# Reordering around three seams of a macaron trunk: weight casts ahead of squares, a scan product ahead of a mix, decay products behind the state sums

## The chip, the core and the metric

The kernel runs on one core of a Trainium2 chip, as one program. The metric is device microseconds of one execution; the time before is the median of three runs. Besides, one execution was recorded by the hardware profiler; its lines are shown below as they were printed.

The engines are called by the profile's names: PE is TensorE's matmuls and PEld its weight loads, DVE is VectorE, ACT is ScalarE, POOL is GpSimd, SP is SyncE, which issues most of the transfers.

## What is computed

Two layers over a sequence of 512 rows of width 1024. Each layer is a macaron: half a SwiGLU, a mixer, half a SwiGLU, each behind an RMSNorm. The mixer of layer 0 is a Mamba-2 SSD, that of layer 1 is an S5 state-space model. A final RMSNorm ends it.

```python
for i in range(2):
    x = x + 0.5 * swiglu(rmsnorm(x, ffn1_norm[i]), ffn1_w_in[i], ffn1_w_out[i])
    h = rmsnorm(x, mix_norm[i])
    m = ssd_mixer(h, ...) if i == 0 else s5_mixer(h, ...)
    x = x + m
    x = x + 0.5 * swiglu(rmsnorm(x, ffn2_norm[i]), ffn2_w_in[i], ffn2_w_out[i])
return rmsnorm(x, final_norm)

# SSD, per chunk, in 8 groups of 4 heads
decay = exp(where(causal, cs[t] - cs[s], -inf))
y_diag = einsum(cb * decay, dtx)
y_off = einsum(c, state) * exp(cs)
new_state = state * exp(cs[-1]) + einsum(b, exp(cs[-1] - cs) * dtx)

# S5: 64 groups of width 16, 64 complex states each
states = scan(lam_bar, b_bar u);  y = Re(c states) + d u
out = (gelu(y) @ W_val + b) * sigmoid(gelu(y) @ W_gate + b)
```

## The kernel before

Activations are kept transposed, eight tiles `xT[d]` of 128 channels by 512 positions. Every float32 product is made from high and low halves: a weight tile of up to 1024 x 128 is fetched to `wst`, ScalarE casts its high half `whi` (L226), VectorE subtracts it for the low half `wlo` (L228), and `proj` issues three matmuls for each 128 rows (L235 to L237). Activations are split the same way into `hH` (L173) and `hL` (L182), or `ah` and `al`. There are three buffers each for `whi` and `wlo`, four for `wst`.

The program runs six stages one after the other: `f1_0`, `ssd`, `f2_0`, `f1_1`, `s5`, `f2_1`. A planner orders the instructions of each engine by the order in which they are written and by its own estimate of when each is ready. Inside a `manual_schedule` region the engines that it names keep the written order; a nested region orders only those that the outer one doesn't. `keep_in_program_order` pins one instruction behind the one written before it on its engine. TensorE is in written order everywhere around the change.

**The feed-forward stage `ffn7`** (`f2_0`, `f1_1`, `f2_1`) takes the 22 tiles of the hidden width in five parts. Each part ends in an output pass over the eight `d`: `part` issues the projection into `pos[d]`, `split` prepares the weight of two steps on, `fetch_to` asks for later ones, and `after(d)` adds half of the result to `xT[d]` (L597, or L594 with `turn`, which writes it transposed for S5). In the last part `after` also calls the next stage's `Prep.take`: it makes `hH` and the square `sq` (L160) on ScalarE, and leaves for one step later (`held`) a `rest` that makes `hL` and adds the square to `acc` (L167) on VectorE. `pop` runs one closure of the list `fill`. In `f1_1` the last eight closures and those left over load and prepare what S5 needs: `scan_ops` (operators `opH` and tables `tb`), `out_ops` (`opP`), `u_load` (the vectors `U`, written out by `s5_sink` and read back regrouped), `res_load` (four gate weights) and `res_w`, which casts (L1381) and subtracts (L1389) such a weight. Then come the sums over channels (L137, or L198 ahead of S5) and the Newton steps of the inverse root (L121 to L128).

In `ffn7` the main loop is in written order on all five engines; the weights split ahead of that loop, and the seam between two stages, are the planner's.

**The SSD stage** treats eight groups `g`; only TensorE is in written order. For each group `states` forms three chunk states: matmuls (L847), a copy (L851), and two times a product with the decay (L853) and a sum (L857). `exps` makes the exponentials on ScalarE (L881), `decay(e)` multiplies them by `cb` on VectorE (L888, once for each pair of heads), and `outp(e)` uses the states (L897) and the decay products (L904) on TensorE. In the last group these steps are run between the steps of `out_rows`, the output projection (L779).

**The S5 stage** has TensorE, SP and GpSimd in written order. Its channels lie in eight blocks `i`. `states(i)` scales `U` by the norm (L1407) and multiplies by `opH` (L1413) into a PSUM tile; `swap(i)` copies its halves crosswise on ScalarE (L1424, L1425); `scan(i)` is three elementwise steps (L1433 to L1435), the scan (L1437), two copies (L1441, L1442) and three more steps (L1443 to L1445) that give `v`; `mix(i, h, w)` multiplies blocks `i` and `i + 1` by `opP` (L1454), with `w = 128` from `U` and with `w = 0` from `v`; `channels(i)` transposes the gelu of the result (L1474) and splits it (L1478, L1479); `glu_k` and `glu_out` are the gate. There are four PSUM tiles `aux` for `states`, `mix` and `channels`.

Of the kernel before, what the change touches and what calls it, by code (L numbers as in the profile page):

```python
# [13 lines left out]
OP = mybir.AluOpType  # L14
AX = mybir.AxisListType

T = 512
D = 1024
KD = 8
# [3 lines left out]
NG = 8  # L23
# [7 lines left out]
def trunk_kernel(ctx, tc, x, ffn1_norm, ffn1_w_in, ffn1_w_out, mix_norm, ffn2_norm, ffn2_w_in, ffn2_w_out,  # L31
# [189 lines left out]

        return split_w(fetch_w(src, kt, eng)[0], kt)

    def split_w(st, kt):
        hi = wpool.tile([128, KD, 128], F32R, name="whi", bufs=3)[:, :kt]
        S.copy(hi, st)  # L226
        lo = wpool.tile([128, KD, 128], F32R, name="wlo", bufs=3)[:, :kt]
        V.tensor_tensor(lo, st, hi.bitcast(F32), op=OP.subtract)  # L228
        return hi, lo

    def proj(ps, w, H, L, first=True, last=True):
        hi, lo = w
# [71 lines left out]
    def ffn7(pr, w_in, w_out, nxt, parts, fill=(), late=None, ring=None, pad=40, turn=None, after_w=(), have=None):  # L304
# [20 lines left out]
        def fetch_to(j):  # L325
            while len(raws) < min(j + 1, len(items)):
                raws.append(fetch_w(*items[len(raws)])[0])

        def split(j):
            if j < len(items) and j not in whole:  # L330
                fetch_to(j)
                whole[j] = split_w(raws[j], items[j][1])

        sevens = list(range(parts[0][1], FT))
        es = ExitStack()
# [197 lines left out]
        with tc.manual_schedule(engines=ALL):  # L533
            todo = []

            def pops(n):
                for _ in range(n):
                    todo and todo.pop(0)()

            for p, (a, b) in enumerate(parts):  # L540
                out = AH, AL = [], []
                prev = None
                for f in range(a, b):
                    if p:
                        iteration(f, prev, b, out)
                        prev = pairs[f]
                        continue
                    pg, pu = mm_ps(), mm_ps()
                    proj(pg, whole[2 * f], pr.H, pr.L)
                    split(2 * f + 2)  # L550
                    fetch_to(2 * f + 5)
                    gt, up = sv.tile([128, T], F32, name="gt"), sv.tile([128, T], F32, name="up")
                    if f == 0:
                        pr.sums()
                    else:
                        pops((0, 1, 2, 2, 2)[f])
                        V.tensor_tensor(gt, pg, pr.rbc, op=OP.mult)
                        S.activation(gt, gt, AF.Silu)
                    proj(pu, whole[2 * f + 1], pr.H, pr.L)
                    split(2 * f + 3)  # L560
                    fetch_to(2 * f + 6)
                    if f == 0:
                        pr.finish()
                        V.tensor_tensor(gt, pg, pr.rbc, op=OP.mult)
                        S.activation(gt, gt, AF.Silu)
                        for k in range(4):
                            todo += build(k)
                    else:
                        pops((0, 2, 2, 2, 0)[f])
                    V.tensor_tensor(up, pu, pr.rbc, op=OP.mult)  # L570
                    gated(up, 1.0, gt, out)
                    pop()
                n = b - a
                last = b == FT
                pos, held = [], []
                steps = {}
                if not last:
                    def step(name):
                        return lambda: getattr(pairs[b], name)()
                    if p == 0:  # L580
                        new_pair()
                        new_pair()
                    steps = {0: ["five"], 3: ["add7", "six"], 4: ["s6", "add3"], 7: ["s12"]}

                def part(d, k0, k1):
                    h, lo = whole[at[p, d]]
                    proj(pos[d], (h[:, k0:k1], lo[:, k0:k1]), AH[k0:k1], AL[k0:k1], first=k0 == 0, last=k1 == n)

                def after(d):
                    pops(1)  # L590
                    if last and turn:
                        new = s5.pop("spare", None) or turn()
                        pv, xv = [a_.rearrange("p (k q) -> p k q", q=8) for a_ in (pos[d], xT[d])]
                        V.scalar_tensor_tensor(new.rearrange("p (q k) -> p k q", q=8), pv, 0.5, xv, op0=OP.mult, op1=OP.add)  # L594
                        s5["spare"], xT[d] = xT[d], new
                    else:
                        V.scalar_tensor_tensor(xT[d], pos[d], 0.5, xT[d], op0=OP.mult, op1=OP.add)  # L597
                    if last:
                        held.append(nxt.take(d, hold=True))
                        if d:  # L600
                            held.pop(0)()
                    for nm in steps.get(d, ()):
                        getattr(pairs[b], nm)()
                    if last:
                        nxt.flush(3)
                    pop()

                for d in range(KD):
                    j = at[p, d]
                    pos.append(mm_ps())  # L610
                    if d == 0:
                        part(0, 0, 1)
                        if prev:
                            prev.acc_u4()
                            prev.c22()
                        split(j + 2)
                        if prev:
                            mul(prev.A, prev.W[3], 6)
                            prev.silu0()
                            prev.silu1()  # L620
                            mul(prev.E, prev.W[4], 0)
                            prev.c21()
                            gated(prev.up, -1.0, prev.gt, out)
                            if last:
                                es7.close()
                                fetch_to(j + 4)
                                if late:
                                    late()
                        part(0, 1, n - 1)
                        continue  # L630
                    if d == 1:
                        part(1, 0, n - 1)
                        for e in range(2):
                            part(e, n - 1, n)
                        split(j + 2)
                        fetch_to(j + 5)
                        for e in range(2):
                            after(e)
                        continue
                    part(d, 0, n)  # L640
                    if d < KD - 1 or last:
                        split(j + 2)
                    fetch_to(j + 5)
                    after(d)
                pops(len(todo))
                if last:
                    held.pop(0)()
            while fill:
                fill.pop(0)()
            nxt.flush()  # L650
            if nxt.kind != "hilo":
                nxt.sums()
                nxt.finish()
# [4 lines left out]
    def ssd(pr, nxt):  # L658
        w_in, w_out = ssd_in_proj[0], ssd_out_proj[0]
        with ExitStack() as es:  # L660
# [147 lines left out]
            def scan(g, BT, CT, XS, SZ):  # L808
# [76 lines left out]
                def decay(e):  # L885

                    m = st["M", e]
                    V.tensor_tensor(m, m, st["cb"][:, None, :].to_broadcast([128, 2, T]), op=OP.mult)  # L888

                def outp(e):  # L890
                    M = st["M", e]
# [500 lines left out]
    def res_w(j):  # L1392
        res_hi(j)
        res_lo(j)

    def s5_stage(pr, nxt):
        with ExitStack() as es:
# [124 lines left out]
            scan_ops(3, 1)  # L1522
            scan_ops(2, 2)
            scan(1)
            for i in (4, 5):
                u_load(i)
                scan_ops(i, 1)
            scan_ops(3, 2)
            out_ops(2, 0)
            scan_ops(4, 2)  # L1530
            states(2)
            for h in range(2):
                mix(0, h, 0)
            states(3)
            swap(2)
            swap(3)
            next_out(2)
# [62 lines left out]
        return rows  # L1600


    op_es = ExitStack()

    def prep_for(st):
        if st is None:
# [107 lines left out]
    for i, s in enumerate(stages[:-1]):  # L1714
# [9 lines left out]
        else:  # L1724
            L = int(s[-1])
            wi, wo = (ffn1_w_in, ffn1_w_out) if s[:2] == "f1" else (ffn2_w_in, ffn2_w_out)
            if s in s5_pre[:1]:
                ffn(pr, wi[L], wo[L], nxt, fill=pre0, ready=ready, done=done, early=early, pad=160)
                pre_es.close()
            elif s in s5_pre:  # L1730
                with tc.manual_schedule(engines=MAN):
                    have = ffn7(pr, wi[L], wo[L], nxt, ((0, 5), (5, 9), (9, 13), (13, 17), (17, 22)),
                                after_w=[(ffn1_w_in[1][:, c:c + 128], KD) for c in (0, FF)])
            elif stages[i + 1] == "s5":
# [4 lines left out]
                    G.memset(s5["sel"].rearrange("p (a b) -> p a b", b=8)[:, :, 7:8], 1.0)  # L1739
                    out_ops(0, 0)  # L1740

                fill = [lambda: None] * 63
                fill[52] = lambda: (scan_ops(0, 2), scan_ops(1, 1))
                fill[53] = lambda: scan_ops(1, 2)
                fill[54] = lambda: out_ops(1, 0)
# [4 lines left out]
                fill[59] = lambda: (res_load(3), res_w(1))  # L1750
                fill[60] = lambda: u_load(2)
                fill[61] = lambda: (u_load(3), res_w(2))
                fill[62] = lambda: res_w(3)
                with tc.manual_schedule(engines=MAN):
                    ffn7(pr, wi[L], wo[L], nxt, ((0, 5), (5, 9), (9, 13), (13, 17), (17, 22)), fill=fill, late=late5, ring=s5["ring"], pad=40,
                         have=have, turn=lambda: s5["op"].tile([128, T], F32, name="xn", bufs=1))
            else:
                def late():
                    fin["p"] = ctx.enter_context(tc.tile_pool(name="fin", bufs=2, side="right"))
# [38 lines left out]
```

## Time and profile before

| | before |
|---|---|
| median of three runs | 2044.01 us (2043.23 to 2044.3) |
| the profiled execution | 2039.9 us |
| its span, first to last instruction | 2038.0 us |
| mean granted TensorE clock | 0.991 |
| busy: TensorE, VectorE, ScalarE, GpSimd | 1988.1, 1493.7, 943.4, 223.9 us |
| HBM read, written | 215.06 MB, 21.04 MB |

The span of the profiled execution is taken from the profiler's records; its own time is taken around it, like that of the runs. In a timeline a row has start and duration in us, engine, line, operation, what it writes and reads, shapes, and in brackets the idle time of the engine before it and what released it. In the table by stretches each engine has its busy time and its number of instructions, followed by the granted clock, the share of the transfer engines and GB/s. A line can be that of a helper, so L228 is any weight's low half.

### The profile page before, as it was taken

Reading aid. Unit: us, or ns where it says so; the run is one execution under the profiler, and the core shown is the slowest. Engines: PE = TensorE matmul, PEld = TensorE weight load, DVE = VectorE, ACT = ScalarE, POOL = GpSimd, SP = SyncE. Lnnn points to the kernel's source line nnn. Section 1 sums busy time; section 2 is a strip of 40 time slices with the busy share of each in tenths; the row PEclk is TensorE's granted clock in tenths of the full one; section 3 lists DMA queues with packets and bytes.
Section 4 is the critical chain, followed back from the end, with each engine's and each line's share of the span. In section 5 each row is a group of like instructions: output and inputs, shape, how many; then the busy total and the mean of one; then the engine's idle time right before and its main releaser. Section 6 shows DMA issues by size and latency. Waiting matters only on the chain. (4 is left out here: it accounts for less than half of the span.)

```text
span 2038.0 us, 32117 instructions
## 1 busy us (share of the span) xinstructions
PE 1988.1 (98%) x12477; PEld 1727.5 (85%) x12477; DVE 1493.7 (73%) x2677; ACT 943.4 (46%) x1613; POOL 223.9 (11%) x338
## 2 busy tenths in 40 slices
PE   8999999999999999999999999999996999999997
PEld 7887778888888887889999978999985888999996
DVE  6899995688885787776677677677768657866675
ACT  5324334465663555434444534454444433444453
POOL 1002332012111010000111000001101100100010
PEclk9999999999999999999999999999997999999999
DMA  7436676344333332455566336446767432654561
GB/s 183 127 120 170 161 193 136 93 113 125 110 107 112 99 93 62 115 133 119 138 152 151 86 92 157 114 124 147 177 184 259 134 95 80 163 136 114 129 142 66
DMA packets 410057, 265.47 MB, mean 130 GB/s; under 512 B 40008, under 2 KB 383088, under 8 KB 409904
## 3 DMA queue, kind: packets, MB, share of 16 engines
q1 hardware_dynamic: 383024, 202.60, 35.5%
q0 software_dynamic: 26560, 59.75, 14.1%
q8 instruction: 98, 1.61, 0.3%
q10 hardware_dynamic: 320, 1.06, 0.1%
q14 instruction: 55, 0.45, 0.1%
HBM read 215.06 MB, written 21.04 MB: 116 GB/s over the span
## 5 line engine op out<-in xcount | busy, mean ns | idle before, releaser
L226 ACT CAST whi<-wst 128x1024 fp32r<-128x1024 f32 (+3 forms) x354 | 315.5, 893 | 373.7 <-PE mm L236 290.6
L228 DVE TENSOR_TENSOR wlo<-wst,whi 128x1024 fp32r<-128x1024 f32 (+3 forms) x354 | 364.1, 1029 | 120.8 <-ACT whi L226 119.0
L235 PE MATMUL mm<-hH,whi 128*128 128x512 f32 x984 | 389.9, 396 | 0.0
L236 PE MATMUL mm<-hL,whi 128*128 128x512 f32 x984 | 384.8, 391 | 1.8 <-DVE hL L182 1.7
L237 PE MATMUL mm<-hH,wlo 128*128 128x512 f32 x984 | 383.8, 390 | 0.0
L237 PE MATMUL mm<-ah,wlo 128*128 128x512 f32 x704 | 274.8, 390 | 0.0
L235 PE MATMUL mm<-ah,whi 128*128 128x512 f32 x704 | 274.5, 391 | 0.0
L236 PE MATMUL mm<-al,whi 128*128 128x512 f32 x704 | 274.4, 390 | 0.0
L236 PEld LDWEIGHTS mm<-hL,whi 128*128 128x128 f32 x984 | 185.1, 188 | 40.8 <-DVE hL L182 3.0
L235 PEld LDWEIGHTS mm<-hH,whi 128*128 128x128 f32 x984 | 185.0, 188 | 39.8 <-issue 1.8
L237 PEld LDWEIGHTS mm<-hH,wlo 128*128 128x128 f32 x984 | 185.0, 188 | 39.5 <-issue 0.4
L384 PE MATMUL mm<-th,hH 128*128 128x256 f32 x612 | 173.5, 284 | 0.0
L386 PE MATMUL mm<-th,hL 128*128 128x256 f32 x612 | 173.2, 283 | 0.0
L385 PE MATMUL mm<-tl,hH 128*128 128x256 f32 x612 | 173.1, 283 | 0.0
L237 PEld LDWEIGHTS mm<-ah,wlo 128*128 128x128 f32 x704 | 132.2, 188 | 28.0 <-issue 0.6
L236 PEld LDWEIGHTS mm<-al,whi 128*128 128x128 f32 x704 | 132.3, 188 | 26.5 <-issue 0.2
L235 PEld LDWEIGHTS mm<-ah,whi 128*128 128x128 f32 x704 | 132.3, 188 | 26.1
L299 POOL DMA_DIRECT2D wu<-wst x51 | 43.1, 846 | 827.5 <-DMA wst<-in_ffn_w_in_dram 384.4
L384 PEld LDWEIGHTS mm<-th,hH 128*128 128x128 f32 x612 | 117.4, 192 | 2.4 <-ACT up L458 2.4
L385 PEld LDWEIGHTS mm<-tl,hH 128*128 128x128 f32 x612 | 117.4, 192 | 0.0
L386 PEld LDWEIGHTS mm<-th,hL 128*128 128x128 f32 x612 | 117.4, 192 | 0.0
L385 PE MATMUL mm<-tl,whi 128*128 128x256 f32 x408 | 115.5, 283 | 0.0
(393 smaller groups left out, 3917.6 us busy)
## 6 DMA issues: line engine op xcount, KB each, us to landing
wst<-in_ffn_w_in_dram SPq DMA_DIRECT2D x125, 512.0 KB, 4.6
wu<-in_ffn_w_in_dram SPq DMA_DIRECT2D x51, 512.0 KB, 5.9
wst<-in_ssd_in_proj_dram SPq DMA_DIRECT2D x48, 512.0 KB, 4.0
wst<-in_ffn_w_out_dram SPq DMA_DIRECT2D x72, 256.0 KB, 2.9
wst<-in_ffn_w_out_dram SPq DMA_DIRECT2D x48, 320.0 KB, 3.2
wu<-wst POOLq DMA_DIRECT2D x51, 256.0 KB, 4.5
ws<-wst POOLq DMA_DIRECT2D x51, 256.0 KB, 4.8
dec<-d_cs POOLq DMA_DIRECT2D x16, 512.0 KB, 4.8
```

What stands on the lines that cost most here:

```text
L226: S.copy(hi, st)
L228: V.tensor_tensor(lo, st, hi.bitcast(F32), op=OP.subtract)
L235: PE.matmul(ps, hi[:, k], H[k], start=first and k == 0, stop=False)
L236: PE.matmul(ps, hi[:, k], L[k], start=False, stop=False)
L237: PE.matmul(ps, lo[:, k], H[k], start=False, stop=last and k == n - 1)
L299: G.dma_start(dst, src, accum_op=OP.add)
L384: PE.matmul(ps[:, c0], hi[:, k], mh, start=first and k == 0, stop=False, skip_group_check=True)
L385: PE.matmul(ps[:, c0], hi[:, k], ml, start=False, stop=False, skip_group_check=True)
L386: PE.matmul(ps[:, c0], lo[:, k], mh, start=False, stop=k == 3, skip_group_check=True)
```

## The change

It has four parts.

`split_w` is divided into `split_hi` and `split_lo`, and inside `ffn7` `split` into `high` and `low`. In the last part's output pass `high` stands where `split` stood, and `low` behind the addition to `xT` and `take`. At `d == 1` two weights are cast, one with each of the two calls of `after`. With `turn` (in `f1_1`), the `rest` of step 6 runs ahead of the addition of step 7.

One region with all five engines is opened ahead of `f2_0` and closed behind `f1_1`.

In S5 the product `states(3)` is written ahead of the two `mix(0, h, 0)`, and `res_w(3)` is written behind `scan(1)` instead of in the last closure of `f1_1`.

In the SSD stage both decay products of the first and the last group are pinned behind what is written before them on VectorE: for the first product of a group that is the last sum of its states.

```diff
-    def split_w(st, kt):
+    def split_hi(st, kt):
         hi = wpool.tile([128, KD, 128], F32R, name="whi", bufs=3)[:, :kt]
         S.copy(hi, st)
+        return hi
+
+    def split_lo(st, hi, kt):
         lo = wpool.tile([128, KD, 128], F32R, name="wlo", bufs=3)[:, :kt]
         V.tensor_tensor(lo, st, hi.bitcast(F32), op=OP.subtract)
         return hi, lo
+
+    def split_w(st, kt):
+        return split_lo(st, split_hi(st, kt), kt)
...
+        halves = {}
+
+        def high(j):
+            if j < len(items) and j not in whole and j not in halves:
+                fetch_to(j)
+                halves[j] = split_hi(raws[j], items[j][1])
+
+        def low(j):
+            if j in halves:
+                whole[j] = split_lo(raws[j], halves.pop(j), items[j][1])
+
         def split(j):
-            if j < len(items) and j not in whole:
-                fetch_to(j)
-                whole[j] = split_w(raws[j], items[j][1])
+            high(j)
+            low(j)
...
-                def after(d):
+                def after(d, j=None):
                     pops(1)
+                    if d == KD - 1 and last and turn:
+                        held.pop(0)()
                     if last and turn:
...
                     if last:
                         held.append(nxt.take(d, hold=True))
-                        if d:
+                        low(j)
+                        if len(held) > 1:
                             held.pop(0)()
...
                         for e in range(2):
                             part(e, n - 1, n)
-                        split(j + 2)
-                        fetch_to(j + 5)
+                        if not last:
+                            split(j + 2)
+                            fetch_to(j + 5)
                         for e in range(2):
-                            after(e)
+                            high(j + 2 + e)
+                            if e == 0:
+                                fetch_to(j + 5)
+                            after(e, j + 2 + e)
                         continue
                     part(d, 0, n)
-                    if d < KD - 1 or last:
+                    if last:
+                        high(j + 2)
+                    elif d < KD - 1:
                         split(j + 2)
                     fetch_to(j + 5)
-                    after(d)
+                    after(d, j + 2)
...
                     m = st["M", e]
-                    V.tensor_tensor(m, m, st["cb"][:, None, :].to_broadcast([128, 2, T]), op=OP.mult)
+                    i = V.tensor_tensor(m, m, st["cb"][:, None, :].to_broadcast([128, 2, T]), op=OP.mult)
+                    if g in (0, NG - 1):
+                        tc.keep_in_program_order(i)
...
             scan_ops(2, 2)
             scan(1)
+            res_w(3)
...
             states(2)
+            states(3)
             for h in range(2):
                 mix(0, h, 0)
-            states(3)
             swap(2)
             swap(3)
...
             elif s in s5_pre:
+                region.enter_context(tc.manual_schedule(engines=ALL))
                 with tc.manual_schedule(engines=MAN):
                     have = ffn7(...)
...
-                fill = [lambda: None] * 63
+                fill = [lambda: None] * 62
...
-                fill[62] = lambda: res_w(3)
                 with tc.manual_schedule(engines=MAN):
                     ffn7(...)
+                region.close()
```

More of the change, by code (lines that the diff above doesn't have):

```diff
@@ L1600, in fin_sink @@
         return rows
-    op_es = ExitStack()
+    op_es, region = ExitStack(), ExitStack()
     def prep_for(st):
```

## The prediction

> **What bounds the kernel now.** I read the page first, then TensorE's waits, then the timelines of single engines around each wait.
>
> ```profile
> PE 1988.1 (98%) x12477; PEld 1727.5 (85%) x12477; DVE 1493.7 (73%) x2677; ACT 943.4 (46%) x1613; POOL 223.9 (11%) x338
> ...
> PE aux L1454 <- DVE v L1445: 12.4, 4, 4.9
> PE aux L1413 <- DVE U L1407: 5.8, 1, 5.8
> PE aux L897 <- DVE st L857: 4.1, 3, 2.0
> ...
> PE aux L198 <- POOL v L1440: 2.2, 1, 2.2
> PE mm L236 <- DVE hL L182: 1.7, 2, 1.4
> ```
>
> The columns of the waits are total us, times, longest. TensorE is busy for 98% of the span, so only its idle time, or time at a lowered clock, can be won without removing matmuls, and the change removes none. The five rows hold 26.2 us. All of them lie at the four places that the edits touch: L897 in the SSD stage, L236 where `f2_0` meets `f1_1`, L198 and L1413 where `f1_1` meets S5, L1454 inside S5. I go through them in that order.
>
> **Part 1, the pinned decay products (L888).** Rows of TensorE, then VectorE, then two stretches with the granted clock (the column after POOL):
>
> ```profile
> 455.70 0.49 PE L897 MATMUL aux<-CT,st 128*128 128x128 f32 x2 [1.50 <-DVE st L857]
> ...
> 787.80 0.49 PE L897 MATMUL aux<-CT,st 128*128 128x128 f32 x2 [0.61 <-DVE st L857]
> 790.27 0.68 PE L897 MATMUL aux<-CT,st 128*128 128x128 f32 x2 [1.98 <-DVE st L857]
> 790.87 1.98 PE L904 MATMUL aux<-dec,dtx 128*64 128x128 f32 x16
> ...
> 794.14 1.09 PE L904 MATMUL aux<-dec,dtx 128*64 128x128 f32 x16
> ...
> 448.61 1.23 DVE L888 TENSOR_TENSOR dec<-dec,cb 128x1024 f32<-128x1024 f32 x1 [0.27 <-issue]
> 449.75 0.42 DVE L851 COPY st<-aux 128x256 f32<-128x256 f32 x1
> ...
> 784.39 0.42 DVE L853 TENSOR_TENSOR st<-st,decS 128x256 f32<-128x256 f32 x1
> ...
> 786.19 1.23 DVE L888 TENSOR_TENSOR dec<-dec,cb 128x1024 f32<-128x1024 f32 x1 [0.78 <-ACT dec L881]
> 787.33 0.42 DVE L857 TENSOR_TENSOR st<-st,aux 128x256 f32<-128x256 f32 x1
> ...
> 789.80 0.42 DVE L857 TENSOR_TENSOR st<-st,aux 128x256 f32<-128x256 f32 x1
> 790.90:792.90 2.00, 2.00 (x18) 1.67 (x17) 0.55 (x1) 0.00 (x0) 0.00 (x0) 0.50 0.47 139
> 792.80:794.30 1.50, 1.50 (x10) 1.38 (x10) 0.80 (x2) 0.00 (x0) 0.00 (x0) 0.65 0.00 0
> ```
>
> A decay product takes 1.23 us and the state operations 0.42 us each. In the first group the second product stands just ahead of the first state copy; in the last group it stands, with its own 0.78 us wait, between a state's product (784.39) and its sum (787.33). Pinned behind the last sum, both products leave the state chain. First group: TensorE waits 1.50 us; the chain can begin 1.1 us earlier (449.75 less 448.61) and has nothing of 1.23 us in it; gain between 0 and 1.50, taken at 1.50. Last group: three state operations are left after 784.39, 1.3 us, so the last sum can be done by about 786 where TensorE asks for it from 787; gain 0.61 + 1.98 = 2.59. After the 1.98 us the clock was 0.50, then 0.65: 16 matmuls took 1.98 us instead of 1.09 (0.89), and 1.5 us at 0.65 lost 0.53. I count these 1.4 us as won too. What is late next: the products themselves. The moved 2 x 1.23 us are due when L904 begins, in the last group at 788 and two us later; from 786 the two end at about 788.5, so the first has no slack to speak of and the second about 1.5 us. If the planner lets other work of VectorE in ahead of the last sum, that sum comes at 787.5, the first product at 788.7 instead of 787.8, and the last group wins 2.6 or more with part of the clock; so bounds are 2.5 and 4.0, and I take 4.0, since everything that VectorE must do before 788 fits. For the first group the lower end is 0 because its two products are due 2 us apart, and 2.46 us of VectorE could end as late as the state sums do now; nothing makes it lose, since the stretch ends on the same work.
>
> [...]
>
> **Part 2, one region of fixed order over `f2_0` and `f1_1`, and the casts in the last output pass.**
>
> ```profile
> 1183.55 0.50 PE L236 MATMUL mm<-hL,whi 128*128 128x512 f32 x1 [1.42 <-DVE hL L182]
> ...
> 1178.61 1.23 DVE L228 TENSOR_TENSOR wlo<-wst,whi 128x1024 fp32r<-128x1024 f32 x1 [0.99 <-ACT whi L226]
> 1179.76 0.69 DVE L597 SCALAR_TENSOR_TENSOR xT<-mm,xT 128x512 f32<-128x512 f32 x1
> ...
> 1181.62 1.22 DVE L228 TENSOR_TENSOR wlo<-wst,whi 128x1024 fp32r<-128x1024 f32 x1
> 1182.75 0.75 DVE L182 SCALAR_TENSOR_TENSOR hL<-xT,cols,hH 128x512 fp32r<-128x512 f32 x1
> ```
>
> VectorE's last L597 stood behind a weight's low half that waited 0.99 us for its cast. In the change L597 comes first, and the low half follows the squares. The second low half, of a weight of `f1_1`, was let in ahead of `hL`; one region keeps it behind. `hL` then comes over 2 us earlier (1.22 and 0.99), more than the 1.42 us for which TensorE waits. The gain is 1.4. Bounds: 0, and 1.7, the whole row of the waits (its other 0.3 us is a second wait, in another stage). A loss would need a low half that TensorE is short of: those that now come behind L597 belong to the weight two steps on, and the one between is already split, so a step of 15 or more matmuls covers them. In the step `d == 1` two weights are cast instead of one; the loads keep their order on SP, and GpSimd issues nothing there, so no transfer is moved past another. The same loop ends `f2_1`; no row of the waits names its lines there, and I count 0 with that as the reason. The region also fixes the order of ScalarE, GpSimd and SP from `f2_0` to `f1_1`; both stages' inner loops were in written order already, so only the seam between them changes.
>
> **Part 3, the end of `f1_1`: acc ahead of the last xT, and `res_w(3)` moved out.** TensorE, VectorE, ScalarE:
>
> ```profile
> 1525.50 0.39 PE L237 MATMUL mm<-ah,wlo 128*128 128x512 f32 x1
> 1528.05 1.97 PE L198 MATMUL aux<-acc,sel 128*128 128x64 f32 x16 [2.16 <-POOL v L1440]
> 1529.85 1.95 PE L198 MATMUL aux<-sq,sel 128*128 128x64 f32 x16
> ...
> 1526.28 1.03 DVE L594 SCALAR_TENSOR_TENSOR xT<-mm,xT 128x512 f32<-128x512 f32 x1
> 1527.15 0.79 DVE L167 TENSOR_TENSOR acc<-acc,sq 128x512 f32<-128x512 f32 x1
> ...
> 1532.51 1.29 DVE L1389 TENSOR_TENSOR hL<-wst,hH 128x512 fp32r<-128x512 f32 x2 [2.64 <-ACT hH L1381]
> 1533.72 0.22 DVE L121 TENSOR_SCALAR nw_v<-aux 128x64 f32<-128x64 f32 x1
> ...
> 1536.87 2.50 DVE L1407 TENSOR_TENSOR U<-U,nw_y 128x512 f32<-128x512 f32 x4
> ...
> 1527.40 0.63 ACT L160 ACTIVATE sq<-xT 128x512 f32<-128x512 f32 x1 [0.84 <-DVE xT L594]
> ...
> 1531.86 1.14 ACT L1381 CAST hH<-wst 128x512 fp32r<-128x512 f32 x2 [2.80 <-DMA wst<-in_s_glu_w_dram]
> ```
>
> TensorE's wait of 2.16 us is put down to GpSimd, but what ended last is `acc` at 1527.94. With `acc` done before the last xT, the first 16 sums can begin when the projection ends, 1525.89; the last square is there by 1528.0 as now (1527.40 and 0.63), when the second 16 want it, 1.97 us after the first. The sums end at 1529.8, not 1531.80. The Newton steps began only at 1533.72, because the low half of the fourth gate weight (1532.51, 1.29 us, behind a cast that waited for its transfer until 1531.86) stood ahead of them. Moved away, they begin at 1529.9: 3.8 to 3.9 us earlier, and TensorE's L1413 with them. Bounds are 0, if something else stands in that place on VectorE, and 3.9, and I take 3.9, since nothing but the sums is left in the written order ahead of the steps. The vectors U that L1407 reads come by transfers on SP, the fourth of them last; L1407 takes them one by one, and `states(0)` needs only the first. The moved `res_w(3)` issues no DMA, so SP keeps its queue. The cost is 1.29 us on VectorE and 1.14 us on ScalarE somewhere in S5.
>
> **Part 4, `states(3)` ahead of `mix(0)`.** TensorE, ScalarE, VectorE:
>
> ```profile
> 1553.87 3.43 PE L1454 MATMUL aux<-opP,v 128*64 128x128 f32 x29 [4.91 <-DVE v L1445]
> ...
> 1557.13 1.79 PE L1413 MATMUL aux<-U,opH 128*64 128x64 f32 x30
> ...
> 1559.01 0.58 ACT L1424 COPY z<-aux 64x512 f32<-64x512 f32 x1 [0.86 <-PE aux L1413]
> ...
> 1556.10 0.68 DVE L1443 TENSOR_TENSOR v<-z,tb 128x504 f32<-128x504 f32 x1
> 1560.22 0.69 DVE L1433 TENSOR_TENSOR z<-aux,tb 128x512 f32<-128x512 f32 x1 [3.44 <-ACT z L1425]
> ...
> 1544.00:1554.00 10.00, 0.86 (x8) 0.45 (x6) 9.73 (x15) 4.88 (x7) 2.16 (x5) 0.71 1.00 335
> ```
>
> In the stretch 1544 to 1554 VectorE is busy 9.73 of 10 us and TensorE 0.86: S5 runs at VectorE's pace here. VectorE's one large hole is the 3.44 us before 1560.22: `states(3)` (1557.13) stood in TensorE's queue behind `mix(0)`, which waited for `v`; its copies (1559.01) then held ScalarE. Ahead of `mix(0)`, `states(3)` falls into TensorE's 4.91 us wait, and the hole closes: 3.44 us. Against it I charge the moved 1.29 us, since VectorE has no other hole to put it in: net 2.15. `states(3)` itself issues no transfer that isn't out already (its `U` and `opH` are asked for before the step), and behind it in TensorE's queue waits only `mix(0)`, which can't start before 1553.87 anyway. Late next is `v` for the third and fourth products, still VectorE's. Bounds: 0 (the transfers' share is already 1.00 in that stretch) and 3.44 plus the time that L1454 lost at the lowered clock, which I leave at some 1.5.
>
> **The sum.** 1.5 + 4.0 + 1.4 + 3.9 + 2.15 = 12.95, say 13.0 us. It is taken from the profiled execution, 2039.9 us (span 2038.0), so 2026.9 there; the median of the runs is 2044.01, 4.1 us above that execution, and the forecast is for the median: 2031.0.
>
> **The rivals.**
> - The moved product floats back. VectorE and ScalarE are not in written order in S5, so the planner may put the cast and low half of the fourth weight where it thinks their load has landed. The load landed at 1531.84, after the new end of the sums (1529.8). Ahead of the Newton steps, the 3.9 us are gone but the 1.29 us too: 10.4, 2033.6. With the cast ahead of the last square on ScalarE, the square comes at 1533.0 and the second sums end at 1535.5, 1.8 us later than the Newton start of now: 8.6, 2035.4. For it: in S5 the planner fills each hole. Against: the planner may count the load's queue correctly. Chance 0.28.
> - S5 is held by its transfers, and closing VectorE's hole only shows the next wait: share 1.00 speaks for it; 9.73 of 10 us of VectorE against. 13.0 less 2.15: 2033.2. Chance 0.12.
> - [...] Chance 0.05.
> - Slower: the order of the middle six SSD groups is the planner's, and with two groups pinned it may place their products or states as badly as the last group has them now, 4.0 us each. Two to three such groups leave a gain within 4 us; 3.25 use up the 13.0; all six give 13.0 - 24 = 11 us slower, 2055. Against it: TensorE waits on L857 three times only, all in the two groups pinned. Chance 0.06 for no change, 0.04 for slower.
>
> **How the numbers follow.** Forecast 0.45, then 0.28, 0.12, 0.05, 0.06, 0.04. About 0.2%, 4.1 us, is what a measurement of this kernel can tell from no change. The first four cases lie below 2039.9: faster 0.90; same 0.06; slower 0.04. Low end: the upper bound of part 4 (2.8 more) and a little more clock, 4 us below 2031.0, 2027. High end: past 2035.4, to where one group's 4.0 is lost on top, 2039.
>
> **What the changed profile would show.** No L897 wait on L857 over 0.3 us, clock 1.00 after the last group, and both L888 behind their last L857. `hL` ahead of the next weight's low half, no L236 wait of 1.4 us. L198 starting within 0.2 us of the last projection, and the Newton steps within 0.2 us of the last L198 with no L1389 ahead of them; if L1389 is there, the first rival holds. VectorE's L1433 for the fourth product straight behind its scan, no 3.44 us hole. The prediction is wrong if new waits on L904 or L146 appear in the middle groups, or if TensorE's wait on L1445 before `mix(2)` grows by what was won.

## The result and the profile after

The changed kernel takes 2029.21 us (median of four runs, 2028.56 to 2029.34) against 2043.62 us (2040.74 to 2044.3) beside it; the ratio is 0.9931, 95% interval 0.9915 to 0.9947. Its profiled execution took 2029.28 us with a span of 2027.4 us at a mean clock of 0.993. The spans of the two profiled executions differ by 10.65 us, their medians by 14.4, because the runs of before scatter: in 31 runs of four jobs they lie from 2037.82 to 2044.7 us, those of the changed kernel, 14 runs in three jobs, from 2027.85 to 2029.89. The profiled execution of before was among its shorter ones. What follows about the change as a whole is read from the two traces, so it has 10.65 us to account for.

The page's first row, then TensorE's waits in the kernel after (total us, times, longest):

```profile
PE 1985.7 (98%) x12477; PEld 1726.1 (85%) x12477; DVE 1495.0 (74%) x2677; ACT 943.7 (47%) x1613; POOL 223.4 (11%) x338
...
PE aux L1440 <- DVE U L1434: 7.1, 1, 7.1
PE aux L1481 <- DVE v L1472: 6.7, 4, 3.5
PE aux L1440 <- DVE z L1460: 2.8, 1, 2.8
PE aux L1481 <- issue: 1.9, 1, 1.9
PE aux L931 <- DVE dec L913: 0.8, 2, 0.4
PE mm L242 <- DVE hL L182: 0.3, 1, 0.3
```

L1440 is L1413 of before, L1481 is L1454, L924 and L931 are L897 and L904, L913 is L888, L1408 and L1416 are the cast and the low half of a gate weight (L1381, L1389). In the experiments the numbers behind an edit shift by a few. Gone from the list are L924's 4.1 us behind the states, L198's 2.2 and 1.4 of L242's. The longest row is where the prediction failed: TensorE waits at the start of S5 for 7.1 us, where before it waited for 5.8.

I followed every TensorE instruction through both traces and noted how much earlier it comes after the change:

| stretch | earlier at its start | at its end | won there | predicted |
|---|---|---|---|---|
| start of the program | 0 | -0.97 | -1.0 | none |
| first SSD group | -0.97 | 0.36 | 1.3 | 1.5 |
| middle SSD groups | 0.36 | 0.33 | 0 | 0 |
| last SSD group | 0.33 | 4.55 | 4.2 | 4.0 |
| seam of `f2_0` and `f1_1` | 4.54 | 6.62 | 2.1 | 1.4 |
| end of `f1_1`, to S5's first matmul | 6.62 | 7.40 | 0.8 | 3.9 |
| S5 | 7.40 | 10.65 | 3.3 | 2.15 |

Nowhere else does it change by more than 0.1. The first row isn't the change's doing. All versions give TensorE the same work there, and in their traces it arrives ahead of the first SSD group anywhere between 444.97 and 446.55 us. In this execution the second load of the input came 0.3 us later than in that of before, and the matmuls went from 0.43 to 0.23 us apart at about 14.1 us instead of 12.2. So two executions are compared here by the time that each needs for a stretch, not by when it gets there. Without that row the edits won 11.6 us.

Now the rows of the changed kernel that stand for these places. The SSD groups, on TensorE and VectorE, and the stretches of the last group with the granted clock behind POOL:

```profile
452.92 1.23 DVE L231 TENSOR_TENSOR wlo<-wst,whi 128x1024 fp32r<-128x1024 f32 x1 [2.29 <-ACT whi L226]
454.06 0.41 DVE L882 TENSOR_TENSOR st<-st,aux 128x256 f32<-128x256 f32 x1
454.39 2.35 DVE L913 TENSOR_TENSOR dec<-dec,cb 128x1024 f32<-128x1024 f32 x2
...
455.76 1.09 PE L931 MATMUL aux<-dec,dtx 128*64 128x128 f32 x16 [0.40 <-DVE dec L913]
...
784.27 0.68 DVE L804 TENSOR_TENSOR xT<-mm,xT 128x512 f32<-128x512 f32 x1
784.87 1.22 DVE L913 TENSOR_TENSOR dec<-dec,cb 128x1024 f32<-128x1024 f32 x1
786.00 0.41 DVE L882 TENSOR_TENSOR st<-st,aux 128x256 f32<-128x256 f32 x1
786.34 1.22 DVE L913 TENSOR_TENSOR dec<-dec,cb 128x1024 f32<-128x1024 f32 x1
...
787.70 1.09 PE L931 MATMUL aux<-dec,dtx 128*64 128x128 f32 x16 [0.39 <-DVE dec L913]
789.00:791.00 2.00, 2.00 (x24) 1.67 (x24) 2.00 (x5) 0.00 (x0) 0.00 (x0) 1.00 0.53 155
793.00:796.00 3.00, 3.00 (x15) 2.44 (x13) 2.03 (x4) 1.49 (x3) 0.00 (x0) 1.00 0.00 0
```

In the first group a weight's low half, held for 2.29 us by its cast, was let in ahead of the last state sum, and both products come behind it: a wait of 0.40 us stands where 1.50 stood. In the last group one product came ahead of the last sum (786.00) all the same, the other behind it. The early one is the second pair's: TensorE takes the first pair's first, and waits for the one that ends at 787.56. The second is written behind an addition to `xT` (784.27), so that is what its pin ties it to. The sum is early enough even so, and the clock stays at 1.00. The end of `f1_1` and S5, on TensorE, VectorE and ScalarE:

```profile
1519.11 1.89 PE L198 MATMUL aux<-acc,sel 128*128 128x64 f32 x16
1521.15 2.00 PE L198 MATMUL aux<-sq,sel 128*128 128x64 f32 x16
1530.22 3.35 PE L1440 MATMUL aux<-U,opH 128*64 128x64 f32 x64 [7.07 <-DVE U L1434]
...
1570.84 1.09 PE L1481 MATMUL aux<-opP,U 128*64 128x128 f32 x16 [1.92 <-issue]
...
1524.59 1.14 ACT L1408 CAST hH<-wst 128x512 fp32r<-128x512 f32 x2 [2.47 <-DMA wst<-in_s_glu_w_dram]
...
1525.24 0.69 DVE L1416 TENSOR_TENSOR hL<-wst,hH 128x512 fp32r<-128x512 f32 x1 [2.31 <-ACT hH L1408]
1525.85 0.22 DVE L121 TENSOR_SCALAR nw_v<-aux 128x64 f32<-128x64 f32 x1
1525.98 0.68 DVE L1416 TENSOR_TENSOR hL<-wst,hH 128x512 fp32r<-128x512 f32 x1
...
1548.69 0.68 DVE L1470 TENSOR_TENSOR v<-z,tb 128x504 f32<-128x504 f32 x1
1549.30 0.68 DVE L1460 TENSOR_TENSOR z<-aux,tb 128x512 f32<-128x512 f32 x1
```

The sums start behind the projection without a wait and end at 1523.15, but the Newton steps begin at 1525.85: the low half of the fourth gate weight, written far behind them now, stands ahead of and among them again. In S5, VectorE's L1460 for the fourth product follows the work ahead of it directly, the hole of 3.44 us is gone, and a wait of 1.92 us at 1570.84, which no instruction ended, has come up; a transfer into `opP` landed just before, at 1570.68.

### The profile page after: what moved, and what is told of

The parts are those of the page before. It is cut to its first block, busy times and chain, and to the rows that moved or that the text cites. A ratio compares the mean times of both kernels' runs of the same rounds, so it can differ in the third digit from the quotient of the medians.

```text
span 2027.4 us, 32117 instructions
## 1 busy us (share of the span) xinstructions
PE 1985.7 (98%) x12477; PEld 1726.1 (85%) x12477; DVE 1495.0 (74%) x2677; ACT 943.7 (47%) x1613; POOL 223.4 (11%) x338
## 4 chain that ended last, share of the span: by engine, by line
PE 89%; DVE 6%; issue 2%; ACT 2%; DMA 1%; SPq 0%; DVEq 0%; ACTq 0%
PE mm L241 20%; PE mm L242 20%; PE mm L243 20%; PE mm L400 6%; PE mm L401 6%; PE mm L402 6%; PE aux L402 2%; PE aux L401 2%; PE aux L400 2%; DVE cv L780 1%; DVE wlo L231 1%; PE aux L931 1%; DVE z L1464 0%; PE aux L872 0%; PE aux L242 0%
## 5 line engine op out<-in xcount | busy, mean ns | idle before, releaser
L241 PE MATMUL mm<-hH,whi 128*128 128x512 f32 x984 | 390.1, 396 | 0.0
L242 PE MATMUL mm<-hL,whi 128*128 128x512 f32 x984 | 384.9, 391 | 0.3 <-DVE hL L182 0.3
L241 PE MATMUL mm<-ah,whi 128*128 128x512 f32 x704 | 274.5, 391 | 0.0
L242 PE MATMUL mm<-al,whi 128*128 128x512 f32 x704 | 274.4, 390 | 0.0
L241 PEld LDWEIGHTS mm<-hH,whi 128*128 128x128 f32 x984 | 185.3, 188 | 39.9 <-issue 1.6
L242 PEld LDWEIGHTS mm<-hL,whi 128*128 128x128 f32 x984 | 185.3, 188 | 38.7 <-issue 1.2
L242 PEld LDWEIGHTS mm<-al,whi 128*128 128x128 f32 x704 | 132.3, 188 | 26.6 <-issue 0.2
L241 PEld LDWEIGHTS mm<-ah,whi 128*128 128x128 f32 x704 | 132.3, 188 | 26.0
L615 DVE SCALAR_TENSOR_TENSOR xT<-mm,xT 128x512 f32<-128x512 f32 x112 | 77.0, 688 | 65.9 <-PE mm L243 65.9
```

What stands on the lines that cost most here:

```text
L241: PE.matmul(ps, hi[:, k], H[k], start=first and k == 0, stop=False)
L242: PE.matmul(ps, hi[:, k], L[k], start=False, stop=False)
```

## The experiments

Each time is the median of five runs. The changed kernel, run again twice as a control, took 2029.06 and 2028.46 us.

> The changed kernel itself, as the measure for the three others beside it. Every theory: within 1 us of 2029.2.

> The changed kernel as it is, the control of this call: 2029.1, with a spread of 1 us.

**The decay products of the last group float again.**

```diff
-                    if g in (0, NG - 1):
+                    if g == 0:
```

> The changed kernel, but the decay products of the last SSD group are not pinned; those of the first are. Theory (a wait is worth its idle time plus the clock lost behind it): TensorE's two waits on the state sums near 787 us come back, 2.6 us, and the clock falls to half behind them for about 3.5 us, 1.4 us more; less the 0.4 us that TensorE now waits for a decay product: 3.7 us slower than the changed kernel, about 2033. [...] Rival 2 (the planner finds another order for the group anyway): within 1 us of the changed kernel.

Measured 2032.72 us (2031.89 to 2034.17), 3.5 us above the changed kernel. TensorE's rows, and stretches as above:

```profile
789.45 0.80 PE L924 MATMUL aux<-CT,st 128*128 128x128 f32 x2 [1.98 <-DVE st L882]
790.18 1.98 PE L931 MATMUL aux<-dec,dtx 128*64 128x128 f32 x16
...
789.00:791.00 2.00, 1.55 (x10) 1.32 (x12) 0.95 (x3) 0.00 (x0) 0.00 (x0) 0.50 0.69 195
793.00:796.00 3.00, 3.00 (x21) 2.42 (x21) 1.33 (x3) 0.00 (x0) 0.00 (x0) 0.53 0.00 0
```

The wait of 1.98 us and the clock of 0.50 are back together, and the price is more than the idle time, 0.60 + 1.98 = 2.58 us. The profiled execution, the slowest of the five, shows even 5.4 us more between 775 us and the end of `f2_0`. So the last group's pin carries 3.5 us or more, the clock's share with it.

**The decay products of the first group float again.**

```diff
-                    if g in (0, NG - 1):
+                    if g == NG - 1:
```

> The changed kernel, but the decay products of the first SSD group are not pinned; those of the last are. Theory: the wait of 1.50 us on the state sums near 455 us comes back and the one of 0.40 us on a decay product goes: 1.1 us slower, about 2030.3, clock 1.00 all the while. Rival: the planner shifts the six groups behind it too, and the sum comes out 2 us or more to either side.

Measured 2029.54 us (2028.65 to 2030.74). TensorE's waits show the 1.5 us back:

```profile
PE aux L924 <- DVE st L882: 1.5, 1, 1.5
```

Yet the median rose by 0.3 us. The trace shows why that is too little: this execution reached the group 0.54 us earlier than that of the changed kernel. By the time that TensorE needs from ahead of the group (445 us) to the end of the group it takes 13.29 us here, as before the change, and 11.96 to 11.98 in all twelve traces with the pin. To 725 us it takes 279.6 us here and before the change, 278.5 to 278.9 in the twelve. So the pin is worth 1.3 us in the group, of which some 0.3 are lost again by 520 us, and 0.7 to 1.2 us remain: the theory's 1.1.

**Without the region over both stages.**

```diff
-                region.enter_context(tc.manual_schedule(engines=ALL))
...
-                region.close()
```

> The changed kernel without the region over f2_0 and f1_1 (the inner loops keep their own). Theory: the addition to xT ahead of the low half already won the seam; the next weight's low half, let in again ahead of the last hL, moves that from 1175.3 to 1176.4 us, and TensorE wants it by about 1177.0: a wait of 0.3 us at most, 2029.2 to 2029.5. Rival: the region is what won it, and TensorE's wait on hL of 1.4 us comes back: 2030.6 or more.

Measured 2028.62 us (2028.12 to 2030.2). VectorE:

```profile
1175.13 1.22 DVE L231 TENSOR_TENSOR wlo<-wst,whi 128x1024 fp32r<-128x1024 f32 x1
1176.26 0.75 DVE L182 SCALAR_TENSOR_TENSOR hL<-xT,cols,hH 128x512 fp32r<-128x512 f32 x1
```

The next weight's low half is ahead of `hL` again, and no wait of TensorE on it is listed; its matmuls come through the seam 0.28 us later than in the changed kernel. With the casts in the new order `hL` has nearly that much slack. Beside them the region is worth 0.3 us at most, less than the medians can tell.

**The old order of the casts, region kept.**

```diff
-                        low(j)
...
-                    if last:
-                        high(j + 2)
-                    elif d < KD - 1:
+                    if last or d < KD - 1:
                         split(j + 2)
```

> The casts of the output passes go back to the order of before (a weight's low half straight behind its cast, ahead of the addition to xT); the region over both stages, the early acc sum and all else stay as after. Control beside it (the changed kernel again): 2029.1. Before had two delays of hL at the seam of f2_0 and f1_1, 0.99 us (the low half that waited for its cast) and 1.22 us (the next weight's low half let in ahead), and TensorE waited 1.42 us. Theory, two delays that add, either remedy being nearly enough by itself: the region still keeps the next low half behind hL, 0.2 us of wait is left, within 0.7 us of the control. Rival, the order of the casts alone wins the seam: the wait of 1.4 us is back, 2030.5 to 2030.8.

Measured 2030.45 us (2028.47 to 2032.26), 2.0 us above its control: the theory's 0.7 is exceeded, but not at the place that the rival names. VectorE, then TensorE and a stretch with the granted clock:

```profile
1177.60 0.74 DVE L182 SCALAR_TENSOR_TENSOR hL<-xT,cols,hH 128x512 fp32r<-128x512 f32 x1
1178.67 1.23 DVE L231 TENSOR_TENSOR wlo<-wst,whi 128x1024 fp32r<-128x1024 f32 x1 [0.33 <-ACT whi L226]
...
1518.37 1.29 DVE L1414 TENSOR_TENSOR hL<-wst,hH 128x512 fp32r<-128x512 f32 x2 [0.75 <-ACT hH L1406]
...
1178.40 0.50 PE L242 MATMUL mm<-hL,whi 128*128 128x512 f32 x1 [0.28 <-DVE hL L182]
1522.28 2.03 PE L198 MATMUL aux<-acc,sel 128*128 128x64 f32 x12 [1.57 <-POOL rh L1447]
1524.00:1526.00 2.00, 2.00 (x11) 2.00 (x11) 1.29 (x2) 0.89 (x2) 0.00 (x0) 0.50 1.12 350
```

The region does keep `hL` ahead of the next low half, and the wait there is 0.28 us, not 1.4. Against the control the stretch lost 0.9 us, where before the change it took 2.1 more: either remedy alone wins more than half of the seam. The larger part, 1.6 us up to S5's first matmul, is lost at the end of `f1_1`, which neither theory named: in the old order VectorE comes to a gate weight's low half too early, waits 0.75 us for its cast, and the last `acc` sum is late. L198 then waits 1.57 us, and from 1524 us the clock is 0.50.

**`res_w(3)` back in the last closure.**

```diff
-                fill = [lambda: None] * 62
+                fill = [lambda: None] * 63
...
+                fill[62] = lambda: res_w(3)
```

> The changed kernel, but res_w(3) is back in the last closure of f1_1, as before the change. Theory: moving it in the program moved nothing on the chip, since the planner put its subtractions ahead of and among the Newton steps again, where they wait for the same transfer: within 0.4 us of the changed kernel, 2028.8 to 2029.6. Rival (the prediction): the move is worth 3.9 us less 1.3: 2.6 us slower, about 2031.8.

Measured 2028.71 us (2027.81 to 2029.71), no change. VectorE:

```profile
1524.22 1.29 DVE L1416 TENSOR_TENSOR hL<-wst,hH 128x512 fp32r<-128x512 f32 x2 [2.69 <-ACT hH L1408]
1525.43 0.22 DVE L121 TENSOR_SCALAR nw_v<-aux 128x64 f32<-128x64 f32 x1
```

Both written places give the same order on VectorE. Moving the call, by itself, moved nothing.

**The early `acc` sum taken out.**

```diff
-                    if d == KD - 1 and last and turn:
-                        held.pop(0)()
```

> The acc sum of step 6 goes back behind the last xT of f1_1; all else as after. Control: 2029.1. Theory: L198 starts some 2.2 us later, but the Newton steps are held until 1525.9 by the low half of the fourth gate weight, and the sums would end at 1525.4: within 0.7 us of the control. Rival, the early acc sum carries the gain at this place: 2.2 us slower, 2031.3.

Measured 2029.88 us (2028.52 to 2029.93), 1.4 above its own control and 0.8 above the other. TensorE, then VectorE:

```profile
1520.43 1.97 PE L198 MATMUL aux<-acc,sel 128*128 128x64 f32 x16 [1.94 <-POOL v L1465]
1522.23 1.95 PE L198 MATMUL aux<-sq,sel 128*128 128x64 f32 x16
...
1524.55 1.29 DVE L1414 TENSOR_TENSOR hL<-wst,hH 128x512 fp32r<-128x512 f32 x2 [2.43 <-ACT hH L1406]
1525.76 0.22 DVE L121 TENSOR_SCALAR nw_v<-aux 128x64 f32<-128x64 f32 x1
```

Counted from the last projection of `f1_1`, L198 starts 2.1 us later than in the control, S5's first matmul only 0.05 us. The trace sides with the theory; the medians lie between the two, and what they hold beyond the trace is not assigned. The early sum buys time that the gate weight then takes away.

**The two subtractions of `res_w(3)` pinned behind `scan(1)`.**

```diff
-            V.tensor_tensor(lo[i], st[:, 4 * i:4 * i + 4], hi[i].bitcast(F32), op=OP.subtract)
+            ins = V.tensor_tensor(lo[i], st[:, 4 * i:4 * i + 4], hi[i].bitcast(F32), op=OP.subtract)
+            if pin:
+                tc.keep_in_program_order(ins)
...
-            res_w(3)
+            res_hi(3)
+            res_lo(3, pin=True)
```

> The changed kernel, with the two subtractions of res_w(3) pinned behind scan(1) on VectorE, so that the planner can't put them ahead of the Newton steps. Theory: the Newton steps begin at the end of the sums, 1523.2 instead of 1525.9, and none of their places is taken by a subtraction (0.6 us): U is scaled 3.1 us earlier. The two subtractions, 1.3 us, now lie in the stretch that VectorE sets: 1.8 us faster than the changed kernel. Rival: S5 is held by the queue of its transfers, which ends at the same time, and the start comes earlier for nothing: within 0.7 us.

Measured 2027.06 us (2025.42 to 2029.08), 2.0 us faster than the control. TensorE, VectorE, and two stretches:

```profile
1520.07 1.97 PE L198 MATMUL aux<-acc,sel 128*128 128x64 f32 x16 [1.35 <-POOL rh L1451]
1521.87 3.57 PE L198 MATMUL aux<-sq,sel 128*128 128x64 f32 x16
...
1525.48 0.23 DVE L121 TENSOR_SCALAR nw_v<-aux 128x64 f32<-128x64 f32 x1 [1.99 <-PE aux L198]
1520.00:1522.00 2.00, 1.94 (x17) 1.97 (x18) 0.93 (x1) 0.98 (x2) 0.52 (x3) 0.98 0.70 181
1522.00:1524.00 2.00, 2.00 (x12) 2.00 (x11) 1.29 (x2) 0.68 (x2) 0.00 (x0) 0.50 1.00 345
```

The Newton steps now wait for the sums alone. The profiled execution is the slowest of the five: its second gate weight came late (the cast waited 1.47 us for the transfer, in the control not at all), TensorE idled 1.35 us ahead of L198, and the second 16 sums took 3.57 us at a clock of 0.50 in place of 2.00. The other four are 2 to 3.7 us shorter.

**The same subtractions pinned in the middle of the scalings of `U`, behind `states(1)`.**

```diff
...
             for i in range(2):
                 states(i)
+            res_hi(3)
+            res_lo(3, pin=True)
...
             scan(1)
-            res_w(3)
```

> res_w(3) is written behind states(0) and states(1), its two subtractions pinned there on VectorE; the decay products stay as after. Control: 2029.1. Theory: the Newton steps begin behind the sums, 3.7 us earlier than after, and the 1.29 us of the moved product stand between two scalings of U in their place, where TensorE has work: 3.0 us faster, 2026.1, so that of the 4.1 us that the version with both edits won, 1.1 are the decay products'. Rival: the place of the pin makes no difference to the one behind scan(1), 2.0 us faster, 2027.1, and the decay products carried the other 2.1.

Measured 2024.85 us (2024.57 to 2026.18): 3.6 us faster than its control, 0.9919 of before (0.9906 to 0.9932). VectorE and TensorE:

```profile
1521.91 0.22 DVE L121 TENSOR_SCALAR nw_v<-aux 128x64 f32<-128x64 f32 x1 [0.25 <-PE aux L198]
1526.28 1.29 DVE L1416 TENSOR_TENSOR hL<-wst,hH 128x512 fp32r<-128x512 f32 x2
...
1525.81 3.69 PE L1442 MATMUL aux<-U,opH 128*64 128x64 f32 x64 [3.94 <-DVE U L1436]
```

The Newton steps start right behind the sums (1519.88 + 2.00 = 1521.88 in this trace), and the low half stands in the stretch where TensorE has 3.69 us of matmuls. S5's first matmul comes 3.25 us earlier than in the control. The theory said 3.0, the rival 2.0.

**This pin, both decay products of the last group together behind its last sum, and the first group's states at a high priority.**

```diff
-  both(urgent if g == NG - 1 else states, *[ex1] * (g > 0), lambda: decay(0)), lambda: decay(1),
+  both(urgent if g in (0, NG - 1) else states, *[ex1] * (g > 0), lambda: decay(0), *[lambda: decay(1)] * (g == NG - 1)),
+  (lambda: None) if g == NG - 1 else (lambda: decay(1)),
```

> A version made to beat both: the changed kernel with the subtractions of res_w(3) pinned behind the scaling of the first two U (there VectorE has a hole of 1.47 us later on, so they should cost nothing), the second decay product of the last SSD group put behind the first instead of behind an addition to xT, and high priority for the first group's states. Theory: 3.1 us in S5 and 0.4 us in the SSD stage, 3.5 us faster than the changed kernel. Rival (transfers hold S5): 0.4 to 1 us faster.

Measured 2024.94 us (2024.71 to 2025.73), 4.1 us faster than its control, 0.9929 of before (0.9917 to 0.9941). VectorE and TensorE:

```profile
784.07 0.41 DVE L882 TENSOR_TENSOR st<-st,aux 128x256 f32<-128x256 f32 x1
784.40 2.35 DVE L913 TENSOR_TENSOR dec<-dec,cb 128x1024 f32<-128x1024 f32 x2
...
786.43 1.09 PE L931 MATMUL aux<-dec,dtx 128*64 128x128 f32 x16
```

Both products now follow the last sum and L931 no longer waits, worth 0.4 us by the matmul times of the two versions; in the first group the wait of 0.40 us stays. Nearly all of the 4.1 us is the pin of the gate weight. These two versions are the fastest run here.

**`states(3)` behind `mix(0)` again.**

```diff
-            states(3)
             for h in range(2):
                 mix(0, h, 0)
+            states(3)
```

> The changed kernel with states(3) behind mix(0) again. Theory (the hole in VectorE comes back): VectorE waits 3.4 us for the copies of swap(3); the changed kernel gained 3.4 us inside S5 by the traces, so 2.2 to 3.4 us slower, 2031.4 to 2032.6. Rival (the transfers hold S5, and the hole was filled for nothing): within 0.7 us.

Measured 2030.45 us (2029.07 to 2031.01), 1.4 us above the control: between the theory and the rival. VectorE and TensorE:

```profile
1551.50 0.69 DVE L1460 TENSOR_TENSOR z<-aux,tb 128x512 f32<-128x512 f32 x1 [2.09 <-ACT z L1452]
...
1555.74 1.20 PE L1481 MATMUL aux<-opP,U 128*64 128x128 f32 x16 [2.34 <-issue]
```

The hole is back with 2.09 us. Counted from S5's first matmul, TensorE reaches the product that stands at 1570.84 in the changed kernel after 42.44 us here, after 40.62 to 41.17 in the three traces of the changed kernel, so 1.3 to 1.8 us later. On the way there the three differ more: the one shown above ran at a clock of 1.00 from 1556 to 1560, came to the gate (L241) 2.5 us before the other two, and then waited the 1.92 us, by the time of the landing for `opP`. The two controls ran at 0.50 from 1558 to 1560 and had no such wait; `opP` landed at 1571.09 in the first, and its product began at 1571.80.

## Why the prediction was right, and where it wasn't

The total was near: 13.0 us forecast, 10.65 between the traces or 11.6 without the start of the program, 2031.0 forecast against a median of 2029.21. That it was so near is in part luck: one term came 3.1 us short, the seam and S5 together brought 1.8 more than forecast, and the median fell by 14.4, more than the traces show.

**The last SSD group: 4.0 forecast, 4.2 in the traces, 3.5 in the medians when undone.** Right in size: without the gap the clock stayed at 1.00, with it 0.50 came back, so nothing speaks for the case given 0.05, a clock at half there whatever the gap. The step "both products leave the state chain" was wrong for one of the two, which came ahead of the last sum (784.87), pinned to an addition to `xT`; there was room for it. The wait of 0.39 us at L931 is the "first has no slack" that the prediction named, unpriced.

**The first group: 1.5 forecast, 1.3 in the group, about 1.0 by 725 us.** The upper bound was the better end, though not all of it came. The pin fixes only what stands behind the sum; the planner let another instruction, a low half with a wait of 2.29 us, in ahead of it, and L931 now waits 0.40 us for the products. That some 0.3 us are lost again by 520 us was not forecast; in the two traces above as much comes back by 777 us, where TensorE waits for ScalarE (L146).

**The seam: 1.4 forecast, 2.1, above the upper bound of 1.7.** The mechanism was right, the size too small: the term counted the listed wait of 1.42 us alone. TensorE lost more there: in the trace of before the matmul at the wait comes 1.82 us after the one ahead of it, against 0.22 in the changed kernel, and three beside it (1181.15, 1181.49, 1183.89) come 0.34 to 0.47 us after theirs, against 0.23. The credit is mostly the casts': the region can go at a loss of 0.3 us. With the old casts the region does more than half of the work, so the two remedies overlap and neither has a price of its own. That the new order of casts also serves the end of `f1_1` was not foreseen.

**The end of `f1_1`: 3.9 forecast, 0.8.** Even that may be chance: from a matmul 12.7 us ahead of the last one of `f1_1` to S5's first, TensorE needs 24.81 us before the change, 24.03 after it, and 23.39 to 24.74 in six other traces of versions that differ elsewhere only. The failed step is "Moved away, they begin at 1529.9", with its reason that nothing but the sums is left in the written order ahead of the Newton steps. In S5 the written order doesn't bind VectorE, and the two places of `res_w(3)` give the same order. This is the first rival, given 0.28: the sums end earlier and the Newton steps still wait for a transfer. Its total, 10.4 us, even fits the traces better than the forecast's 13.0; the median, 2029.21, lies nearer to the forecast's 2031.0 than to its 2033.6. The forecast's own mechanism was sound, which the pin shows: with it the steps start 0.03 us behind the sums and the median falls by 3.6 us.

**`states(3)`: 2.15 forecast, 1.4 when undone.** The hole closed as forecast. The charge of 1.29 us for the moved product was not due, because the product never moved. The rival on transfers shows in one of three executions: where TensorE ran at a clock of 1.00 from 1556 to 1560 it waited 1.92 us, by the time of the landing for `opP`, and in the two controls it did not. S5 as a whole is 3.3 us shorter between the traces; the part beyond `states(3)` is not assigned to a cause.

No new wait appeared in the middle SSD groups, so the rival that would have ended slower did not come about. Undone one by one, the edits cost 3.5, 0.3, 2.0, 0.8 to 1.4 and 1.4 us in the medians, some 8 to 9 in all, with the first group's 0.3 nearer to 1.0 by the traces; the rest of the 10.65 may be pairs like the region and the casts, where one covers for the other. That was not tried.

Open is why before scatters over 7 us and the changed kernel over 2. The runs give a hint only: beside the last control, the two runs of before under 2039 us had a mean clock of 0.992, the seven above 2040 us 0.987 to 0.990.

## What to carry to other kernels

Before counting on a moved call, see whether the engine keeps the written order at both ends of the move; where it doesn't, only a pin moves the instruction, and a pin says what stands ahead of it, not what else may come between. Put an instruction that waits for a transfer where the next engine already has work, here between two scalings while TensorE had 3.69 us of matmuls. Undo each edit alone before crediting it: of the named edits two, the region and the moved call, were worth next to nothing here. And where an effect is smaller than the scatter of whole runs, take from several traces the time between two instructions that frame it: the first group's 1.3 us stood clear there and was lost in the medians.

## What the hardware showed

The length of one idle stretch doesn't settle what the clock does in these traces. TensorE idled 1.94 us ahead of L198 in the version with the late `acc`, and the next 32 sums ran at a clock of 1.00 (1.97 and 1.95 us); it idled 1.35 us at the same place in the version pinned behind `scan(1)`, and the clock was 0.50 from about 1522, 3.3 us after the idle stretch began (1518.7). With the old casts it idled 1.57 us there, and the clock was 0.50 from 1524. What else decides it, no run here shows.
